# A hybrid retention and window-attention layer on one core: new queue figures in the order's planner, one store for each retention output, two x blocks held in SBUF, query and key rows in one DRAM array

## The chip, the core and the metric

The kernel runs on one core of a Trainium2 chip. Its time is device time in microseconds (us) for one execution. Three timed runs of the kernel before gave 704.1, 706.53 and 708.13 us, so its median is 706.53 us. The profile comes from one further execution.

## The reference, cut to what matters

```python
def reference(x, norm_w, w_in, ret_norm_w, q_norm_w, k_norm_w, sinks, rel_bias, w_out):
    h = rms_norm(x, norm_w)                                  # x: 1 x 2048 x 1024, float32
    proj = einsum('bsd,de->bse', h, w_in)                    # 2816 columns
    rq, rk, rv, rg, sq, sk, sv, sg = split(proj, [256, 256, 512, 512, 512, 128, 128, 512])
    rq, rk = rotary(rq), rotary(rk)                          # 4 heads of 64
    ro = retention(rq, rk, rv)                               # 4 heads, 128 values each, decay gamma per head
    ro = group_norm(ro) * ret_norm_w * silu(rg)
    so = sliding_window_attention(sq, sk, sv, q_norm_w, k_norm_w, sinks, rel_bias)   # window 128
    so = so * silu(sg)
    return x + einsum('bse,ed->bsd', concat([ro, so]), w_out)

def retention(q, k, v):                                      # by chunks, state carried along
    scores = (q_c k_c^T) * decay
    out = scores v_c + (q_c * xi) state
    state = gamma^C * state + (k_c * zeta)^T v_c
```

Everything is float32, and the output has the shape of x.

## The kernel before, in words

**The four large products.** The projection is cut into three column groups (1024, 768 and 1024 columns) and the output projection is the fourth product. A float32 operand is split into a high part and a remainder (tiles `hi` and `lo`, in the profile `x<-x` and `w<-w`: ScalarE makes the high part, VectorE the remainder), and TensorE does three passes on the parts. Each product goes by a seven-product scheme (`STEPS`, m = 1 to 7) over eight pairs of 128-token chunks, so one projection is 7 x 8 blocks of 4 x 3 matmuls, 672 in all. In the profile they are `acc<-w,x`, with 512 columns of the moving operand, 384 in the second projection.

**What lies between them.** The second, third and fourth product share TensorE with the window attention (`window`, `attend`, `values`) and the retention (`retention`, `keys_of`, `update`, `retain`, `group_norm`), whose plain float32 matmuls are the `m<-...` rows. The names that matter below: `qT` and `ks` are queries and keys of the window attention, `lg` its logits, `pm` the exponentials, `pT` their transposes, `so` its output; `a` is the tile of query and key rows before the rotary step, `qk` and `qkT` what comes of it, `sT` the decayed scores of the retention (VectorE multiplies the scores in PSUM by the mask `dm`), `ro` its outputs; `g` are gate columns, `go` a gated output on its way into the last product. `apart` is a tile rearranged by ScalarE for a transpose by DMA through `planes_dram`.

**What goes through DRAM.** The second projection's rows go to two arrays `rq0_dram` and `rq1_dram` of 384 columns each. `keys_of` reads query and key rows back in two loads (384 columns from the first, 128 from the second). x is loaded from `in_xt` for the first product and its blocks m = 1, 2 and 4 again for the second and third (`kept_blocks`); four sums are kept in `s0_dram` to `s3_dram`. `retain` works on two chunks at once. Its two PSUM banks per head pair are filled so that ScalarE copies each out in one instruction of all 128 partitions (`ro<-m` 128x256); in the tile `ro` half of the rows then belong to the other head and the other half chunk. After the group norm, three stores of 64 partitions for each `ro` tile (one of 256 columns, two of 128) put them in their places in `ro_dram`. Since rows are crossed, the inverse norms are needed crossed too: two small DMAs fill `rstd_crossed`.

**What sets the order.** Every step is recorded by `op` with a cost for each engine that can do it, the buffers that it reads and writes, and a due time in units of blocks of the large products. `Program.emit` then picks step after step: it keeps a time at which each engine is free, a pool of 93 buffers of 128x512 (tag `k`) with a ceiling per use (`SHARE`), and a model of the DMA queue, which is SyncE's (SP, in the planner `Q`). The order that comes out is written into the program for each engine and holds on the chip, however long a step takes there: an instruction that waits keeps back all that stand behind it on its engine, on SP too. In the program each DMA on SP waits, besides what it needs, for the landing of the DMA eight places ahead of it.

The queue's model before: a transfer of `kb` KB takes `0.15 + kb / 450` us of a common bus, lands 2.6 us after that, and the next may be issued after 0.45 us and not before the bus is within `BACKLOG` = 1.5 us:

```python
bus = max(bus, s) + occ
free[e] = max(s + more, bus - BACKLOG)
o.end = bus + lat
```

A buffer that a planned step gives back is used again from the planned end on (`slots`), so a store that lands later than planned holds up the step that gets its buffer next.

Of the kernel before, what the change touches and what calls it, by code (L numbers as in the profile page):

```python
# [29 lines left out]
F32 = mybir.dt.float32  # L30
# [30 lines left out]

AHEAD_OF = {"x": 3.0, "wh": 8.0}
# [23 lines left out]
BACKLOG = 1.5  # L86
# [48 lines left out]
class Program:  # L135
# [33 lines left out]
    def emit(self):  # L169
# [16 lines left out]
        done, now = 0, 0.0  # L186
        while done < count:
            best = None
            for e, found in avail.items():
# [4 lines left out]
                for due, n, o in found[:48]:  # L194
# [13 lines left out]
                    if shared and e != "Q":  # L208
                        s = max(s, port)
# [47 lines left out]
            if e == "Q":  # L257
                occ, lat, more = o.cost[e]
                bus = max(bus, s) + occ
                free[e] = max(s + more, bus - BACKLOG)  # L260
                o.end = bus + lat
            else:
# [50 lines left out]
TURN = (1.8, 2.7, 1.35)  # L313
# [21 lines left out]
def both(n):  # L335
    return {"V": dve(n, True)}
# [21 lines left out]
def dma(kb, issue=0.45):  # L358
    return {"Q": (0.15 + kb / 450, 2.6, issue)}
# [3 lines left out]
VALUES = {P: dma(256, 0.6), 96: dma(192, 0.6), 32: dma(64, 0.63)}  # L363
# [30 lines left out]
def layer(ctx, tc, xt, xfirst, xtok, nw, w_in, w_rn, qkw, sinks, biasg, rope, decays, dmask, gpow, w_out, out):  # L394
# [34 lines left out]
    def fixed(shape, name, dtype=F32):  # L429
        return Buf(name=name, ap=const.tile(shape, dtype, name=name))  # L430
# [56 lines left out]
    rstd_crossed = fixed([P, NCH], "rstd_crossed")  # L487
    crossed = [Part(rstd_crossed, lambda t: t) for _ in range(2)]
    made, held_up = [[], []], Buf(name="held_up", ap=())
# [14 lines left out]
    rq_dram = [scratch([P, 384], f"rq{n}_dram", NCH) for n in range(2)]  # L504
    g_dram = scratch([P, 512], "g_dram", NP)
    ro_rows = dram.tile([NCH, P, 512], F32, name="ro_dram")
    ro_parts = []
    for c in range(0, NCH, 2):
        made_of = [[], []]
        for pr in range(2):  # L510
            at_rows = lambda u, lo, n, c=c, pr=pr: ro_rows[c : c + 2, HALVES[u], pr * 256 + lo : pr * 256 + lo + n]
            made_of[pr].append((Buf(name="ro_dram", ap=at_rows(0, 0, 256).rearrange("k t (x d) -> t k x d", x=2)), HALVES[pr], None))
            for x in range(2):
                made_of[pr].append(
                    (Buf(name="ro_dram", ap=at_rows(1, (1 - x) * P, P).rearrange("k t d -> t k d")), HALVES[1 - pr], x)
                )
        ro_parts.append(made_of)
# [160 lines left out]
    def kept_blocks(base, seq):  # L678
# [6 lines left out]
        for m, p in seq.all:  # L685
            due = base + seq.at[m, p]
            t = kb("x", "raw")
            load(t, of[m](p), due - 2.5)
            B[m, p] = split(t, 512, due - 0.6, "x", "x")
# [187 lines left out]
    def retention(at):  # L877

        for i, half in enumerate(HALVES):
            op(  # L880
                dma(8), lambda e, i=i, half=half: e.dma_start(rstd_crossed()[half, :], rstd_all()[HALVES[1 - i], :]),
                [rstd_all], [crossed[i]], at(0) - 12, label="crossed", also=(rstd_crossed,),
            )
        for t, heads, r in ((0, slice(0, 2), (rstd_all,)), (0, slice(2, 4), tuple(crossed)), (1, slice(0, 4), (rsq_all,))):
            by = rstd_crossed if len(r) == 2 else r[0]
            part = Part(factors[t], lambda a, heads=heads: a[:, :, heads])
            made[t].append(part)
            op(
                {"V": (0.25, 0.33, True)},
                lambda e, part=part, by=by, t=t, heads=heads: e.tensor_tensor(  # L890
                    part(), dec()[:, t : t + 1, heads].to_broadcast([P, NCH, heads.stop - heads.start]),
                    by().unsqueeze(2).to_broadcast([P, NCH, heads.stop - heads.start]), ALU.mult,
                ),
                [dec, *r], [part], at(0) - 9, label="factors", also=(factors[t],),
            )
        op(
            {"V": (0.25, 0.33, True)}, lambda e: e.tensor_tensor(squares(), factors[0](), factors[0](), ALU.mult),
            made[0], [squares], at(0) - 9, label="factors",
# [779 lines left out]
```

## Time and profile before

| | before |
|---|---|
| timed runs, us | 704.1, 706.53, 708.13 (median 706.53) |
| the profiled execution's own time, us | 703.36 |
| its span, first to last instruction, us | 701.6 |
| mean granted TensorE clock | 0.995 |
| TensorE matmul busy, us (share) | 685.6 (98%) |
| VectorE, ScalarE, GpSimd busy, us | 604.6, 475.5, 42.5 |
| HBM traffic | 106.64 MB read, 56.69 MB written |

1.7 us of the execution's own time lie outside the span. "Busy" of TensorE is the union of the matmuls' durations, which overlap, so the 16.0 us of the span that are left are time in which no matmul was in flight. One line number, 390, stands for nearly all instructions, because a helper records them; groups are told apart by their tiles. A row `A <- B` in the view of waits says that engine and tile A were released last by B.

### The profile page before, as it was taken

The numbers are of one execution on the slowest core, as the hardware profiler recorded it, in microseconds if no ns is written. First come the engines' busy times: TensorE is split into PE (matmuls) and PEld (weight loads), VectorE is DVE, ScalarE is ACT, GpSimd is POOL, SyncE is SP. The second block draws the span as 40 slices with busy tenths as digits, with TensorE's granted clock in tenths as the row PEclk, the third lists the DMA queues.
The fourth block names the chain that finished last, engine by engine and source line by source line (L and its number), as shares of the span: only waits on it lengthen the run. The fifth ranks groups of instructions, "written<-read, shape, count | busy, mean of one in ns | idle before, by whom it ended". The sixth has DMA issues, their size and how long they took to land.

```text
span 701.6 us, 15585 instructions
## 1 busy us (share of the span) xinstructions
PE 685.6 (98%) x5428; PEld 578.6 (82%) x5428; DVE 604.6 (86%) x1483; ACT 475.5 (68%) x1122; POOL 42.5 (6%) x75
## 2 busy tenths in 40 slices
PE   9999999999999999999989989999989999999998
PEld 7888888889999999986768767888768788788886
DVE  6999887877999979899988879899787799999962
ACT  7666965656896666979768958995989844253300
POOL 1000000025020001102000000100000000000000
PEclk9999999999999999999999999999989999999999
DMA  9999955989977699999999899699799898315822
GB/s 321 365 342 335 384 179 182 348 270 297 330 194 229 198 302 312 262 323 273 321 268 320 199 266 308 136 269 316 190 316 304 193 290 272 105 45 172 279 102 93
DMA packets 171487, 179.07 MB, mean 255 GB/s; under 512 B 71824, under 2 KB 106768, under 8 KB 171408
## 3 DMA queue, kind: packets, MB, share of 16 engines
q1 hardware_dynamic: 171264, 178.07, 83.9%
q8 instruction: 43, 0.70, 0.4%
q14 instruction: 36, 0.29, 0.1%
q10 hardware_dynamic: 144, 0.00, 0.0%
HBM read 106.64 MB, written 56.69 MB: 233 GB/s over the span
## 4 chain that ended last, share of the span: by engine, by line
PE 75%; DVE 14%; DMA 6%; ACT 2%; issue 2%; SPq 0%; DVEq 0%; ACTq 0%
PE acc L390 64%; PE m L390 10%; DVE x L390 4%; DVE w L390 2%; DVE lg L390 2%; DVE go L390 2%; DMA g<-g_dram 2%; ACT ro L390 1%; DVE t L390 1%; DMA planes_dram<-apart 1%; DVE s L390 1%; DMA w<-in_w_out 1%; DMA x<-s_dram 1%; DMA vd<-aq_dram 1%; DMA so_dram<-so 1%
## 5 line engine op out<-in xcount | busy, mean ns | idle before, releaser
L390 PE MATMUL acc<-w,x 128*128 128x512 f32 (+1 forms) x2700 | 594.9, 379 | 2.2 <-DVE x L390 1.2
L390 PEld LDWEIGHTS acc<-w,x 128*128 128x128 f32 x2700 | 493.7, 189 | 87.1 <-issue 3.2
L390 DVE TENSOR_TENSOR x<-x 128x512 fp32r<-128x512 f32 (+2 forms) x220 | 148.0, 695 | 17.3 <-ACT x L390 17.0
L390 ACT ACTIVATE x<-x 128x512 fp32r<-128x512 f32 (+1 forms) x187 | 111.8, 618 | 15.0 <-DVE x L390 7.2
L390 DVE TENSOR_TENSOR w<-w 128x512 fp32r<-128x512 f32 (+3 forms) x96 | 61.8, 669 | 2.5 <-ACT w L390 2.4
L390 ACT ACTIVATE pm<-lg,nm 128x128 f32<-128x128 f32 x128 | 50.0, 401 | 7.1 <-DVE lg L390 7.1
L390 ACT ACTIVATE w<-w 128x512 fp32r<-128x512 f32 (+1 forms) x72 | 41.0, 603 | 20.2 <-DVE w L390 11.3
L390 DVE CUSTOM_DVE_ANT_0 lg<-m,bias,nsnk 128x160 f32<-128x160 f32 x128 | 42.7, 383 | 8.7 <-PE m L390 8.6
L390 DVE SCALAR_TENSOR_TENSOR w<-w,nw_sb 128x512 fp32r<-128x512 f32 (+3 forms) x72 | 49.1, 706 | 1.0 <-ACT w L390 0.9
L390 DVE TENSOR_TENSOR s<-acc,s 128x512 f32<-128x512 f32 (+1 forms) x64 | 42.1, 657 | 6.9 <-PE acc L390 6.6
L390 POOL TENSOR_SCALAR_AFFINE_SELECT own<-pT 64x512 f32<-64x512 f32 x32 | 25.4, 806 | 258.0 <-ACT pT L390 239.4
L390 DVE TENSOR_TENSOR t<-acc,t 128x512 f32<-128x512 f32 (+2 forms) x33 | 21.2, 642 | 19.9 <-PE acc L390 19.4
L390 ACT ACTIVATE x<-go 128x512 fp32r<-128x512 f32 x40 | 24.2, 626 | 13.7 <-DMA w<-in_w_out 3.6
L390 DVE TENSOR_TENSOR x<-go,x 128x512 fp32r<-128x512 f32 x40 | 27.7, 699 | 3.5 <-ACT x L390 3.5
L390 ACT ACTIVATE s<-acc 128x512 f32<-128x512 f32 (+1 forms) x32 | 17.9, 565 | 18.6 <-PE acc L390 13.6
L390 ACT ACTIVATE w<-w,nw_sb 128x512 fp32r<-128x512 f32 (+3 forms) x44 | 28.2, 682 | 3.0 <-DMA w<-in_w_in 1.8
L390 ACT ACTIVATE apart<-qn 128x1024 uint16<-128x1024 uint16 x16 | 16.9, 1054 | 19.4 <-DVE qn L390 19.3
L390 ACT ACTIVATE ro<-ro,nmu,rg 128x128 f32<-128x128 f32 x64 | 25.2, 486 | 1.1 <-DVE nmu L390 1.1
L390 DVE TENSOR_TENSOR t<-acc,s 128x512 f32<-128x512 f32 (+1 forms) x32 | 21.2, 663 | 5.0 <-PE acc L390 5.0
L390 ACT ACTIVATION_READ_ACCUMULATOR pm<-lg,nm 128x1 f32 x128 | 25.4, 199 | 0.0
L390 ACT ACTIVATE xk<-xk 128x512 f32<-128x512 f32 x32 | 19.9, 623 | 5.9 <-DMA xk<-in_xtok 5.8
L390 PE MATMUL m<-ks,qT 64*32 64x160 f32 x1024 | 23.2, 300 | 0.6 <-issue 0.6
(133 smaller groups left out, 663.6 us busy)
## 6 DMA issues: line engine op xcount, KB each, us to landing
x<-in_xt SPq DMA_DIRECT2D x80, 256.0 KB, 4.8
x<-s_dram SPq DMA_DIRECT2D x64, 256.0 KB, 4.7
planes_dram<-apart SPq DMA_DIRECT2D x56, 256.0 KB, 4.7
w<-in_w_in SPq DMA_DIRECT2D x40, 256.0 KB, 4.8
s_dram<-x SPq DMA_DIRECT2D x32, 256.0 KB, 4.6
xk<-in_xtok SPq DMA_DIRECT2D x32, 256.0 KB, 5.5
res<-in_xtok SPq DMA_DIRECT2D x32, 256.0 KB, 4.4
w<-in_w_out SPq DMA_DIRECT2D x20, 256.0 KB, 5.6
```

The costliest lines, as they stand in the source:

```text
L390: return lambda *a, **k: self.order.put(op(*a, **k))
```

## The change

It has four parts.

- **The queue's model in the planner.** `BACKLOG` goes. A transfer now starts on the bus `FETCH` = 0.3 us after its issue, the queue is held until the transfer eight places ahead has landed (`LANES` = 8), a transfer takes `0.16 + kb / 440` us and lands 2.5 us after, and issuing takes 0.55 us in place of 0.45. The figures of a transpose by DMA change from (1.8, 2.7, 1.35) to (1.6, 2.5, 1.65). These numbers move instructions on every engine.
- **Retention outputs in one transfer.** The matmuls of `retain` use the banks by head (`banks[i]` for `banks[i ^ u]`), with masks and decays laid out to fit. For the second head pair ScalarE crosses the two halves of the partitions while it copies out of PSUM, in four instructions of 64 partitions in place of two of 128. A `ro` tile is stored in one DMA of 128 partitions. `rstd_crossed` and its two DMAs go, and with them one of the small VectorE instructions that make `factors`.
- **Two x blocks kept.** `HELD` = 2: the high and low parts of the first two x blocks of the second projection stay in four of the 93 buffers until the third projection has used them, which then has two loads and two splits fewer.
- **Query and key rows in one array.** `rq0_dram` and `rq1_dram` become one array of 768 columns, and `a` is filled by one load of 512 columns.

```diff
+HELD = 2
+FIRST_X, SPLIT_X = 2.5, 0.6
+SHARE["held"] = 2 * HELD
...
-BACKLOG = 1.5
+LANES, FETCH = 8, 0.3
...
-                    if shared and e != "Q":
+                    if e == "Q":
+                        s = max(s, landings[-LANES] if len(landings) >= LANES else 0.0)
+                    elif shared:
                         s = max(s, port)
...
-                bus = max(bus, s) + occ
-                free[e] = max(s + more, bus - BACKLOG)
+                bus = max(bus, s + FETCH) + occ
+                free[e] = s + more
                 o.end = bus + lat
+                landings.append(o.end)
...
-TURN = (1.8, 2.7, 1.35)
+TURN = (1.6, 2.5, 1.65)
...
-def dma(kb, issue=0.45):
-    return {"Q": (0.15 + kb / 450, 2.6, issue)}
+def dma(kb, issue=0.55):
+    return {"Q": (0.16 + kb / 440, 2.5, issue)}
...
-    rq_dram = [scratch([P, 384], f"rq{n}_dram", NCH) for n in range(2)]
+    rq_rows = dram.tile([NCH, P, 768], F32, name="rq_dram")
...
+            if again and (m, p) in held:
+                B[m, p] = again[m, p]
+                continue
...
-        load(a0, rq_dram[0][c], soon - 3, 192, also=(a,))
-        load(a1, rq_dram[1][c], soon - 3, 64, also=(a,), of=lambda t: t[:, 0:128])
+        op(
+            dma(256), lambda e: e.dma_start(a(), rq_rows[c, :, 0:512]), [rq_dram[0][c], rq_dram[1][c]], [a], soon - 3,
+            label="load a",
+        )
...
-                                    banks[i ^ u][pr]()[HALVES[u ^ pr], k * P : (k + 1) * P], qkT()[r, o : o + 64],
+                                    banks[i][pr]()[HALVES[u ^ pr], k * P : (k + 1) * P], qkT()[r, o : o + 64],
...
-                            h, o = 2 * pr + (u ^ x), (2 * k + pr) * 64
+                            h, o = 2 * pr + x, (2 * k + pr) * 64
...
             for x in range(2):
...
-                op({"A": act(256)}, go, [banks[x][pr]], [ro], due + 0.7, label="ro")
+                for half, to in ((slice(0, P), slice(0, P)),) if pr == 0 else zip(HALVES, HALVES[::-1]):
+                    part = Part(ro, lambda t, x=x, to=to: t.rearrange("p (k x d) -> p k x d", k=2, x=2)[to, :, x, :])
+                    parts.append(part)
+                    op(
+                        {"A": act(256)},
+                        lambda e, part=part, out=banks[x][pr], half=half: e.activation(
+                            part(), out()[half, 0:256].rearrange("p (k d) -> p k d", k=2), AF.Copy
+                        ),
+                        [banks[x][pr]], [part], due + 0.7, label="ro", also=(ro,),
+                    )
...
-            for to, rows, x in ro_parts[c // 2][pr]:
...
-                op(dma(128 if x is None else 64), go, [ro], [to], due + 0.6, label="store ro")
+            store(ro_dram[c // 2][pr], ro, due + 0.6, 280, of=lambda t: t.rearrange("p (k d) -> p k d", k=2))
...
-    B1 = kept_blocks(n7, TWOS)
+    B1 = kept_blocks(n7, TWOS, TWOS.all[:HELD])
...
-    B3 = kept_blocks(2 * n7, TWOS)
+    B3 = kept_blocks(2 * n7, TWOS, TWOS.all[:HELD], B1)
```

TensorE has the same instructions in both programs, in other places. SP has 750 DMAs in place of 802: 32 fewer `ro_dram<-ro`, 16 fewer `a<-rq_dram`, 2 fewer `x<-in_xt` and the 2 of `rstd_crossed`. ScalarE has 16 more `ro<-m` and 2 fewer `x<-x`, VectorE 2 fewer `x<-x`.

The first place is SP's queue near the last retention group, where the gate columns `g` are loaded. Before, the rows are:

```order
L390 DMA ro_dram<-ro 64x2x128 x2
L390 DMA ro_dram<-ro 64x2x256
L390 DMA ro_dram<-ro 64x2x128 x2
L390 DMA_TRANSPOSE r<-planes_dram 128x4x256
L390 DMA go<-ro_dram 128x512 x2
L390 DMA go<-so_dram 128x512
L390 DMA w<-in_w_out 128x512
L390 DMA go<-ro_dram 128x512 x2
L390 DMA w<-in_w_out 128x512 x3
L390 DMA planes_dram<-apart 128x1024
L390 DMA x<-s_dram 128x512
L390 DMA g<-g_dram 128x512
```

Now they are:

```order
L397 DMA w<-in_w_out 128x512
L397 DMA ro_dram<-ro 128x2x256
L397 DMA w<-in_w_out 128x512
L397 DMA_TRANSPOSE r<-planes_dram 128x4x256
L397 DMA ro_dram<-ro 128x2x256 x2
L397 DMA w<-in_w_out 128x512 x2
L397 DMA x<-s_dram 128x512
L397 DMA go<-ro_dram 128x512 x2
L397 DMA g<-g_dram 128x512
L397 DMA planes_dram<-apart 128x1024
L397 DMA go<-so_dram 128x512
L397 DMA go<-ro_dram 128x512 x2
```

Twelve stores of `ro` became four, the four loads of the last product's weights moved ahead of the gate loads, and this `g`, the seventh of eight, stands directly behind the ninth and tenth `go<-ro_dram` instead of eight DMAs later.

The second place is TensorE where the retention begins, early in the third projection; `m<-ks,qT` are logits of the window attention, `m<-ident,pm` transposes of its exponentials, `m<-ident,kn` a transpose of keys. Before, the rows are:

```order
L390 MATMUL m<-v,qk 64x128 x16
L390 MATMUL m<-ks,qT 32x160 x16
L390 MATMUL m<-ident,pm 128x128 x8
L390 MATMUL acc<-w,x 128x512 x3
L390 MATMUL m<-ident,kn 128x128
L390 MATMUL m<-ks,qT 32x160 x16
L390 MATMUL acc<-w,x 128x512 x3
L390 MATMUL m<-ident,pm 128x128 x4
L390 MATMUL acc<-w,x 128x512 x3
L390 MATMUL m<-ident,pm 128x128 x4
L390 MATMUL acc<-w,x 128x512 x30
```

Now they are:

```order
L397 MATMUL m<-v,qk 64x128 x16
L397 MATMUL m<-ks,qT 32x160 x16
L397 MATMUL m<-ident,pm 128x128 x8
L397 MATMUL acc<-w,x 128x512 x21
L397 MATMUL m<-ident,kn 128x128
L397 MATMUL acc<-w,x 128x512 x48
L397 MATMUL m<-state,qkT 64x128 x12
L397 MATMUL m<-qkT 64x64 x16
L397 MATMUL acc<-w,x 128x512 x9
L397 MATMUL m<-v,sT 64x128 x16
L397 MATMUL acc<-w,x 128x512 x15
L397 MATMUL m<-ks,qT 32x160 x16
```

The next group of logits stood 3 matmuls of the large product behind the transposes; now 93 of them lie between.

The third place is ScalarE at one of the retention's copies out of PSUM. Before, the rows are:

```order
L390 ACTIVATE qk<-qk,factors_83 128x64 x4
L390 ACTIVATE apart<-qk 128x1024
L390 ACTIVATE ro<-m 128x2x128 x4
L390 ACTIVATE x<-x 128x512
L390 ACTIVATE w<-w 128x512
```

Now they are:

```order
L397 ACTIVATE qk<-qk,factors_82 128x64 x4
L397 ACTIVATE ro<-m 128x2x128 x2
L397 ACTIVATE ro<-m 64x2x128 x4
L397 ACTIVATE apart<-qk 128x1024
L397 ACTIVATE x<-x 128x512
```

Four copies became six, and here they stand ahead of the rearranging step instead of behind it.

87 lines of the change are left out of this document (32 added, 55 removed).

## Prediction

> **What bounds the kernel now.** I read the page first.
>
> ```profile
> PE 685.6 (98%) x5428; PEld 578.6 (82%) x5428; DVE 604.6 (86%) x1483; ACT 475.5 (68%) x1122; POOL 42.5 (6%) x75
> ```
>
> TensorE is busy for 98% of the span and the change leaves its instructions as they are, so its work is a floor; what can move is the time that it waits, or runs at a lower clock. The view of waits, for TensorE alone, has eight rows:
>
> ```profile
> PE m L390 <- ACT pT L390: 3.9, 2, 2.1
> PE m L390 <- DVE sT L390: 3.3, 1, 3.3
> PE m L390 <- DVE none L390: 1.3, 1, 1.3
> PE acc L390 <- DVE x L390: 1.2, 3, 0.7
> PE acc L390 <- ACT x L390: 1.0, 1, 1.0
> PE m L390 <- DVE go L390: 0.8, 1, 0.8
> PE m L390 <- issue: 0.6, 1, 0.6
> PE m L390 <- ACT pm L390: 0.4, 2, 0.2
> ```
>
> Without the opening (`none`, 1.3) they sum to 11.2 us. Windows of 25 us say where, and what the clock did (columns: window, length, busy time and instructions of PE, PEld, DVE, ACT, POOL, granted clock, DMA share, GB/s):
>
> ```profile
> 50.00:75.00 25.00, 25.00 (x112) 20.71 (x111) 24.67 (x42) 19.14 (x50) 0.00 (x0) 1.00 0.98 340
> 350.00:375.00 25.00, 22.68 (x267) 18.07 (x266) 21.34 (x60) 16.81 (x44) 1.61 (x2) 1.00 1.01 271
> 400.00:425.00 25.00, 22.47 (x342) 17.13 (x333) 19.69 (x74) 15.43 (x36) 1.45 (x2) 1.00 1.04 284
> 500.00:525.00 25.00, 21.36 (x172) 16.85 (x171) 21.32 (x39) 22.02 (x38) 0.00 (x0) 0.87 0.99 286
> 525.00:550.00 25.00, 25.00 (x116) 20.58 (x115) 16.28 (x46) 22.55 (x42) 0.00 (x0) 0.99 0.91 247
> ```
>
> The first product runs without a gap although the DMA engines are as busy there as anywhere. The gaps lie between 325 and 560 us, where attention and retention are slotted in. One of them also lowers the clock: 25 x 0.13 + 25 x 0.01 = 3.5 us of clock are missing around 520 us. About 0.5 us of that fell while TensorE waited anyway, so 3.0 us count. The ceiling of what better order can win is 11.2 + 3.0 = 14.2 us, 2.0%.
>
> Next, what ends each wait last. The largest one, by the chain of waits in a window (start, us, what):
>
> ```profile
> 509.58 6.19 DMA g<-g_dram
> 515.77 0.02 issue
> 515.79 0.03 ACT g L390
> 515.82 0.60 issue
> 516.42 0.72 ACT w L390
> 517.16 0.06 DVE w L390
> 517.83 0.68 DVE t L390
> 518.52 0.66 DVE w L390
> 519.18 0.35 DVE sT L390
> 519.57 1.98 PE m L390 x32
> ```
>
> TensorE needs `sT`. VectorE has its two `sT` behind four `w`, these need ScalarE's `w`, and ScalarE stood for a load of gate columns. The largest wait on `x` and the two on `pT`, these with ScalarE's row ahead, from the timeline (the bracket is the idle time before and its releaser):
>
> ```profile
> 327.27 0.74 PE L390 MATMUL acc<-w,x 128*128 128x512 f32 x2 [1.00 <-ACT x L390]
> 365.62 0.60 ACT L390 ACTIVATE s<-acc 128x512 f32<-128x512 f32 x1 [3.10 <-DMA so_dram<-so]
> 366.76 0.66 PE L390 MATMUL m<-ident,pm 128*128 128x128 f32 x4 [1.76 <-ACT pT L390]
> 412.85 0.60 ACT L390 ACTIVATE pT<-m 128x512 f32<-128x512 f32 x1 [4.78 <-DMA planes_dram<-apart]
> 413.50 1.09 PE L390 MATMUL m<-pT,vs 128*64 128x128 f32 x14 [2.15 <-ACT pT L390]
> ```
>
> At `pT` ScalarE both times got a buffer whose last user was a store that had not landed: the planner took it for free too early. So 3.9 + 3.3 + 0.8 (`go`, a load of `ro_dram`) of the 11.2 us, and the clock's 3.0, go back to DMAs that landed later than planned. The 2.2 us on `x` are another kind; the largest piece is the 1.00 us at 327 us, where logits and exponentials crowd ScalarE and VectorE.
>
> **The queue's figures.** The median times from issue to landing, with the size, of some issues:
>
> ```profile
> a<-rq_dram SPq DMA_DIRECT2D x16, 192.0 KB, 4.6
> ro_dram<-ro SPq DMA_DIRECT2D x16, 128.0 KB, 2.6
> ro_dram<-ro SPq DMA_DIRECT2D x32, 64.0 KB, 2.1
> so_dram<-so SPq DMA_DIRECT2D x16, 256.0 KB, 4.0
> ```
>
> The old model lands 256 KB 0.72 + 2.6 = 3.3 us after issue when idle, and with its backlog of 1.5 us at most about 4.8 us; `g` above took 6.19. The new one lands it after 0.3 + 0.74 + 2.5 = 3.5 us when idle and, with eight in flight, after 8 x 0.74 = 5.9 us. That is nearer. What it is worth: the two waits on `pT` are worth 0 to 3.9 us; I take half, 2.0, since the buffer is again the one with the earliest planned end. The new order has moved 93 matmuls between two groups of logits early in the retention, which thins the crowd behind the 2.2 us on `x`; 0 to 2.2, I take 1.5, as the releasers there are VectorE and ScalarE themselves.
>
> **Retention outputs.** The stores first:
>
> ```profile
> 493.94 7.82 SPq L390 DMA_DIRECT2D ro_dram<-ro  x12
> L390 SPq DMA_DIRECT2D ro_dram<-ro x48: 574/605/1446, 389.2 to 550.9; - x48
> 505.33 0.79 SPq L390 DMA_DIRECT2D go<-ro_dram  x2
> ```
>
> A 64-partition store holds SP for 0.605 us, a load for 0.79 / 2 = 0.4. Of 48 stores 16 remain, so SP is free for 32 x 0.605 = 19.4 us more, and eight of those 32 were in the twelve issued 8 to 16 us ahead of the late `g`. That is 8 x 0.605 = 4.8 us there, and `g` is also eight DMAs earlier relative to the `go<-ro_dram` beside it. If `g` comes in time, ScalarE's wait of 1.5 us goes:
>
> ```profile
> 515.79 0.72 ACT L390 ACTIVATE g<-g,rstd_all 128x512 f32<-128x512 f32 x1 [1.51 <-DMA g<-g_dram]
> ```
>
> TensorE's wait then falls from 3.3 to 1.8 us. What is late next is VectorE's queue of `w` ahead of `sT`, which stands there still. Waits of 1.76 and 2.15 us, above, lie in windows with a clock of 1.00, so at 1.8 the clock's 3.0 us go too: together 4.5 of 6.3, between bounds of 0 and 6.3. The wait on `go` gets 0.5 of its 0.8, because loads of `ro_dram` are no longer behind triples of stores.
>
> The Trainium skill ("TensorE: Matmul & The Clock Gate", HAM oscillation) puts the limit for idle gaps at about 3.4 us, on a free-running window. The wait of 3.28 us here did halve the clock; by the skill as by the rows 1.8 us would not.
>
> ScalarE pays for it:
>
> ```profile
> L390 ACT ACTIVATE ro<-m 128x256 f32<-128x256 f32 x32 | 9.5, 379 | 0.0
> L390 ACT ACTIVATE x<-x 128x512 fp32r<-128x512 f32 (+1 forms) x187 | 111.8, 618 | 15.0 <-DVE x L390 7.2 <-PE acc L390 5.4 <-DVE w L390 1.2
> ```
>
> A copy costs 9.5 / 32 = 0.30 us in a row of them. No 64-partition copy is in the trace; the work per partition is the same 256 elements, so I take 0.30 each, 16 x 0.30 = 4.8 us more, 0.6 for each pair of chunks. It can cost nothing, where TensorE waits for neither `ro` nor what follows, or all 4.8, where it does; no gain, because no copy goes. ScalarE runs 15.4 to 22.6 of 25 us in these windows, and no wait on `ro` stands among TensorE's rows, so I take 1.0. The Trainium skill ("ScalarE: Activation LUTs", Rules for kernel authors) speaks more strongly against the change: about 0.3 us per ACTIVATE and 0.83 ns per element, 0.51 us for each copy and 8.2 us in all as an estimate. By that the term would be 1.7 in place of 1.0. The row has 0.30 us for the whole instruction, and I keep to it. VectorE loses one small instruction and SP two tiny DMAs, worth nothing under the 98%.
>
> **x blocks kept.** Two splits of 111.8 / 187 = 0.6 us on ScalarE, their two remainders on VectorE and two loads go. In this stretch of 125 us in the second projection TensorE has no gap:
>
> ```profile
> 150.00:275.00 125.00, 125.00 (x1265) 118.59 (x1264) 110.38 (x328) 89.83 (x249) 20.16 (x31) 1.00 0.89 264
> ```
>
> So loads and splits of this kind are covered by TensorE's own work. Without that cover two would be worth 2 x 0.6 = 1.2 us, and as they leave shortly ahead of the crowd at 327 us, that much of the 1.5 for `x` may be theirs; I count nothing more. The price is 4 of 93 buffers for the length of the second projection: 0, or one more wait for a buffer of the size of the two above, 2.0; I take 0.5, as there is no wait at all there now.
>
> **One load for `a`.** 16 loads fewer, for 16 x 0.4 = 6.4 us of SP's time. The rotary step waited for both loads before and waits for the one now; 192 KB took 4.6 us and 256 KB of other kinds 4.0 to 6.2. Nothing, within 0.3 either way.
>
> **New waits.** A new order puts new instructions ahead of one another, and the trace of before cannot show which. Its own order, planned by wrong figures, has 3.9 + 3.3 + 1.2 + 1.0 = 9.4 us of waits on `pT`, `sT` and `x`; I take about a fifth of that, 2.0, since half of its causes are the figures that are mended. The bounds are 0 and one wait like that on `sT` with its clock, 6.3.
>
> **The sum.** Against the profiled execution: -2.0 (`pT`) - 1.5 (`x`) - 4.5 (`sT` and clock) - 0.5 (`go`) + 1.0 (copies) + 0.5 (buffers) + 2.0 (new waits) = -5.0, so 703.36 - 5.0 = 698.4 us. The median of the timed runs, 706.53, lies 3.2 above that execution; I carry the difference over and forecast 706.53 - 5.0 = 701.5 us. 0.5% of it, 3.5 us, is about what a measurement of this kernel can tell from no change.
>
> **Rivals.** *The waits only move.* Landing times vary, as 2.1 to 6.2 us in the rows above show, and no fixed figure foresees them; removed waits of 8.5 us come back as others of 4 to 10. For it: five separate places waited before, each for a reason of its own. Against: four of the causes are the same one. Time: 706.53 - 8.5 + 7 + 1.5 = 706.5, within 0.5%. That the held blocks and the single load do nothing belongs here, as they are hidden either way.
>
> *A second clock drop.* The six copies per pair of chunks, ahead of `apart` or `x`, make ScalarE the late one at a `pT` or `x`, in windows where it already ran 22.0 to 22.6 of 25 us. Two copies more, 0.6 us, on top of a wait of 2.15 make 2.75; with one late store it passes 3.3, and from there the clock halves. The price is 3.3 + 3.0 = 6.3 us, and 1.5 for copies and buffers stays. With half of the gains (4.2 of 8.5) the time is 706.53 + 6.3 - 4.2 + 1.5 = 710.1, with a quarter (2.1) 712.2. For it: TensorE's `sT` is still only 6 matmuls behind its scores and VectorE's `w` still ahead of it. Against: SP's 19.4 and 6.4 us of relief lie in this stretch.
>
> **How the numbers follow.** Forecast, faster by over 0.5%: 0.56, with 693 to 703 as its own range. Waits only move: 0.24, at 703 to 710. A second clock drop: 0.20, at 710 to 712.2. Full success is 706.53 - 14.2 = 692.3. The range from 692.5 to 711 leaves out the far half of the last case and next to nothing below. Faster 0.56, same 0.24, slower 0.20.
>
> **What would show it.** Right: no row `PE <- ACT pT` with `DMA planes_dram` or `so_dram` behind ScalarE's idle time; at the last `sT` a wait under 2 us and a clock of 1.00 in every window from 300 to 600 us; SP with 16 rows `ro_dram<-ro`; TensorE's waits after the opening summing to about 6 to 8 us. Wrong: a sum of waits of 11 us or more in other places, a window with a clock under 0.95, or TensorE waiting for `ro` or for a buffer in the second projection. If the copies of 64 partitions take more than 0.4 us each, that term was too small.

## The result, and the profile after

The changed kernel takes 688.6 us (median of four runs, 687.99 to 688.87), the kernel before beside it 705.61 us (704.1 to 708.13): a ratio of 0.9754, interval 0.9722 to 0.9786, or 17.0 us. That is below the forecast of 701.5 us and below the range (692.5 to 711). The profiled execution took 688.87 us, with a span of 687.1 us, 14.5 us less than before. The other 2.5 us of the 17.0 are no gain of that execution: the runs of before have their median 2.2 us above its profile, those of the changed kernel 0.3 us below.

The page's row of busy time, and the three rows that the view of TensorE's waits has in the changed kernel:

```profile
PE 679.3 (99%) x5428; PEld 577.9 (84%) x5428; DVE 604.5 (88%) x1479; ACT 481.5 (70%) x1137; POOL 43.1 (6%) x75
```

```profile
PE m L397 <- ACT pm L397: 2.9, 1, 2.9
PE m L397 <- DVE none L397: 1.3, 1, 1.3
PE acc L397 <- DVE x L397: 0.2, 1, 0.2
```

Seven rows after the opening, 11.2 us, have become two, 3.1 us. That is 8.1 of the 14.5. Most of the rest is in the first row: TensorE's busy time fell from 685.6 to 679.3 us, 6.3 us, for the same 5428 matmuls. The clock does not explain it, as the windows show (columns as in the prediction):

```profile
350.00:375.00 25.00, 24.93 (x402) 20.11 (x395) 24.26 (x99) 20.19 (x65) 3.60 (x4) 1.00 1.11 314
400.00:425.00 25.00, 22.77 (x335) 18.01 (x327) 23.56 (x95) 24.65 (x63) 1.80 (x2) 1.00 0.94 244
425.00:450.00 25.00, 24.14 (x114) 19.72 (x116) 22.03 (x49) 21.54 (x53) 1.55 (x2) 0.86 0.62 193
500.00:525.00 25.00, 25.00 (x205) 20.48 (x204) 23.50 (x59) 24.88 (x43) 0.00 (x0) 1.00 1.11 305
525.00:550.00 25.00, 25.00 (x114) 20.71 (x113) 20.91 (x39) 23.65 (x44) 0.00 (x0) 1.00 1.09 309
```

The gap at 500 to 525 us, which had the largest wait and the low clock, is gone (25.00 busy, clock 1.00). One clock drop remains, at another place: 25 x 0.14 = 3.5 us of clock are missing behind 425 us, as much as before. So the 6.3 us are stalls that the view of waits cannot see. The next row says how they hide: matmuls of the large product, by shape.

```profile
L397 PE MATMUL acc<-w,x 128*128 128x512 f32 x2004 | 467.5, 393 | 0.2 <-DVE x L397 0.2
```

A matmul is shown with 393 ns, but 2004 of them cover 467.5 us, 233 ns each. Each lasts some 160 ns into the next one, so a matmul that starts 160 ns late, or the first 160 ns of any longer stall, leaves no idle time. From both traces I took the time from each matmul's start to the next start, less the median for that pair of tiles and shapes in the same trace, and added up the differences of more than 0.1 us: 30.6 us before, 16.4 us after. These sums hold the waits and the clock's loss too; they differ by 14.2 us, nearly all of the span's 14.5.

The stores, with the time that each holds SP (minimum, median and maximum in ns), and ScalarE's copies:

```profile
L397 SPq DMA_DIRECT2D ro_dram<-ro x16: 359/393/1520, 386.2 to 535.2; - x16
L397 ACT ACTIVATE ro<-m 64x256 f32<-64x256 f32 x32 | 12.1, 379 | 0.6
L397 ACT ACTIVATE ro<-m 128x256 f32<-128x256 f32 x16 | 5.1, 373 | 0.1
```

A store of 128 partitions and 256 KB holds SP for 0.39 us, less than one of 64 partitions and 64 or 128 KB did (0.605). A copy takes 373 or 379 ns by either shape, but in a row those of 128 partitions overlap (before 9.5 us for 32, 0.30 each) and those of 64 do not (12.1 for 32, 0.38 each). ScalarE has 12.1 + 5.1 - 9.5 = 7.7 us more, not 4.8. The Trainium skill's estimate in the prediction (8.2 us, from "ScalarE: Activation LUTs", Rules for kernel authors) comes near that only by chance: its price is that of an ACTIVATE whose bias is a pointer operand, which these copies are not given, and 0.51 us for each copy is not what the row shows.

The wait that remains, by the chain of waits in its window:

```profile
421.81 1.34 ACT pm L397 x7
423.15 0.03 issue
423.18 0.66 ACT ro L397 x2
423.84 0.02 issue
423.86 0.38 ACT ro L397
...
425.04 0.38 ACT ro L397
425.42 0.39 ACT pm L397 x2
425.81 0.04 issue
425.86 1.71 PE m L397 x6
```

TensorE stands for the exponentials `pm`, and between the first four and the next ScalarE makes all six copies of a pair of chunks. The wait is 2.93 us, and the clock halves behind it. This is nearly the mechanism of the rival "a second clock drop" (there the six copies made a `pT` or `x` late, here it is `pm`, and no late store is needed), inside a kernel that is 17 us faster.

### The profile page after: what moved, and what is told of

It reads as the page before. It is cut to its first block, busy times and chain, and to the rows that moved or that the text cites. A ratio compares the mean times of both kernels' runs of the same rounds, so it can differ in the third digit from the quotient of the medians.

```text
span 687.1 us, 15551 instructions
## 1 busy us (share of the span) xinstructions
PE 679.3 (99%) x5428; PEld 577.9 (84%) x5428; DVE 604.5 (88%) x1479; ACT 481.5 (70%) x1137; POOL 43.1 (6%) x75
## 4 chain that ended last, share of the span: by engine, by line
PE 96%; ACT 2%; DVE 1%; DMA 1%; issue 0%; DVEq 0%; ACTq 0%
PE acc L397 83%; PE m L397 13%; ACT ro L397 1%; DMA ro_dram<-ro 1%; DVE lg L397 0%; ACT pm L397 0%; DVE sT L397 0%; DVE x L397 0%; DVE qn L397 0%; DVE tsin L397 0%; ACT w L397 0%; DVE tcos L397 0%; DVE w L397 0%; DVE qk L397 0%; DVE t L397 0%
## 5 line engine op out<-in xcount | busy, mean ns | idle before, releaser
L397 DVE TENSOR_TENSOR x<-x 128x512 fp32r<-128x512 f32 (+2 forms) x218 | 145.7, 690 | 9.4 <-ACT x L397 9.3
L397 ACT ACTIVATE x<-x 128x512 fp32r<-128x512 f32 (+1 forms) x185 | 109.7, 614 | 20.8 <-DVE x L397 16.7
L397 DVE TENSOR_TENSOR w<-w 128x512 fp32r<-128x512 f32 (+3 forms) x96 | 60.4, 653 | 3.2 <-ACT w L397 3.1
L397 DVE TENSOR_TENSOR t<-acc,t 128x512 f32<-128x512 f32 (+2 forms) x33 | 21.1, 639 | 16.6 <-PE acc L397 16.4
L397 ACT ACTIVATE c<-acc 128x512 f32<-128x512 f32 (+1 forms) x24 | 13.4, 560 | 15.9 <-PE acc L397 14.2
L397 DVE TENSOR_TENSOR r<-acc,t 128x512 f32<-128x512 f32 (+1 forms) x32 | 20.8, 651 | 3.5 <-PE acc L397 3.4
```

The costliest lines, as they stand in the source:

```text
L397: return lambda *a, **k: self.order.put(op(*a, **k))
```

## The experiments

Two theories stood against each other at first. *Queue figures*: the planner now knows when DMAs land, so buffers and loads come in time; the stores matter at one or two places. *Stores*: 48 small stores held up everything behind them on SP, and with 16 the order hardly matters. A third came up on the way: *planned price*, that the planner, charged for 48 stores, makes a bad order. All runs, with the kernel before on the same chip (medians of 702.81 to 705.61 us):

| run | queue figures | stores planned / issued | other | median us (range) | ratio, interval |
|---|---|---|---|---|---|
| before | old | 48 / 48 | | 705.61 (704.1–708.13) | 1 |
| changed | new | 16 / 16 | held blocks, one `a` load | 688.6 (687.99–688.87) | 0.9754, 0.9722–0.9786 |
| m1 | new | 48 / 48 | | 714.97 (713.24–716.43) | 1.0172, 1.0135–1.0209 |
| m2 | old | 16 / 16 | held, one load | 697.66 (694.38–700.16) | 0.9919, 0.9891–0.9946 |
| m3 | old | 16 / 16 | | 693.85 (691.9–695.48) | 0.9879, 0.9845–0.9912 |
| m4 | new | 48 / 48 | held, one load | 707.61 (704.38–711.64) | 1.0077, 1.0048–1.0106 |
| m5 | new | 16 / 16 | one load | 687.92 (687.13–689.05) | 0.977, 0.9747–0.9793 |
| m6 | new | 16 / 16 | held | 693.15 (689.55–697.12) | 0.9846, 0.9798–0.9894 |
| m7 | new | 48 / 48 | changed, six copies | 704.82 (702.77–710.87) | 1.0023, 0.9997–1.0048 |
| m8 | old | 48 on GpSimd | | 697.33 (694.87–699.64) | 0.9903, 0.987–0.9936 |
| n1 | new | 16 / 48 | changed | 699.73 (695.68–701.91) | 0.9934, 0.9907–0.9961 |
| n2 | new | 48 / 16 | changed | 700.92 (699.55–702.26) | 0.9948, 0.9921–0.9975 |
| n3 | new | 16 / 16 | | 689.8 (687.67–691.42) | 0.9803, 0.9757–0.9849 |
| `FETCH` 0.35 | new | 16 / 16 | changed | 689.26 (689.14–690.12) | 0.9801, 0.9753–0.9849 |
| n5 | old | 48 / 16 | six copies | 694.18 (692.72–695.87) | 0.9841, 0.9787–0.9894 |
| n6 | new | 16 / 16 | changed, four copies | 684.9 (683.37–685.9) | 0.9706, 0.9654–0.9759 |
| n7 | new | 16 / 16 | changed, copies later | 688.52 (688.19–691.54) | 0.9773, 0.9709–0.9838 |
| n8 | new | 16 / 16 | changed, copies late, old price | 686.93 (686.39–687.29) | 0.9737, 0.9686–0.9787 |
| n9 | new | 16 / 16 | n8 without held blocks | 688.77 (687.06–689.53) | 0.9776, 0.9751–0.9801 |
| n10 | new | 16 / 16 | changed, again | 688.5 (686.18–688.93) | 0.9772, 0.9746–0.9798 |

### Which part carries the gain

m1 is the kernel before with the first part of the change alone, m4 the changed kernel without the second part, m3 the second part alone, m2 the changed kernel without the first:

```diff
# m1, and missing in m2 and m3
-BACKLOG = 1.5
+LANES, FETCH = 8, 0.3
# m3, and missing in m1 and m4
-            for to, rows, x in ro_parts[c // 2][pr]:
+            store(ro_dram[c // 2][pr], ro, due + 0.6, 280, of=lambda t: t.rearrange("p (k d) -> p k d", k=2))
```

> The kernel before with the new queue model alone (48 small stores of the retention outputs, no held blocks, two loads of the query and key rows). Queue theory (the gain comes from an order that fits the landings): two thirds of the gain or more, 691 to 695 us, and no TensorE wait behind a late store. Transfer theory (the gain comes from fewer and larger DMAs): 703 to 707. Chance theory (any new order scatters the waits): anywhere from 688 to 706, with no pattern over the four runs.

> The changed kernel with the old queue model, the other three parts kept. Queue theory: 701 to 707 us, with waits behind DMAs as in the kernel before. Transfer theory: 688 to 693. Chance theory: anywhere from 688 to 706.

> The kernel before with the retention outputs crossed by ScalarE and stored in one DMA, nothing else. Queue theory: 703 to 708 us. Transfer theory: 691 to 697, since 34 of the 52 DMAs go here. Chance theory: anywhere from 688 to 706.

> The changed kernel with the retention outputs as before: four ScalarE copies for each pair of chunks, three stores for each tile. Queue theory: 683 to 690 us, because the wait of 2.9 us behind six copies and its half clock can go. Transfer theory: 698 to 704. Chance theory: anywhere from 688 to 706.

The queue figures alone make the kernel 1.7% slower. The merged stores alone give 8.9 us against the kernel before on their chip (702.81), with the old figures and their old errors; the wait on `sT` does not come back, and 0.3 us on `pT` is left. Without them (m4) the other three parts leave the kernel slower than before. So the theory of the queue figures falls as a cause by itself. But m2 says that the figures are worth something where the stores are merged: 697.66 without, 688.6 with. m1's view of TensorE's waits has one row of a size that no kernel with 16 planned stores has:

```profile
PE acc L393 <- ACT x L393: 15.7, 3, 14.4
```

It lies at 583 us, at the start of the last product, and m4 has its like, 9.1 us at 576.

m5 drops the held blocks, m6 goes back to two arrays and two loads for `a`:

```diff
# m5
-    B1 = kept_blocks(n7, TWOS, TWOS.all[:HELD])
+    B1 = kept_blocks(n7, TWOS)
# m6
-            dma(256), lambda e: e.dma_start(a(), rq_rows[c, :, 0:512]), [rq_dram[0][c], rq_dram[1][c]], [a], soon - 3,
+        load(a0, rq_dram[0][c], soon - 3, 192, also=(a,))
+        load(a1, rq_dram[1][c], soon - 3, 64, also=(a,), of=lambda t: t[:, 0:128])
```

> The changed kernel with HELD = 0: the third projection loads and splits all its x blocks. Store theory (the 48 small stores of the retention outputs, and the order planned around them, cost nearly all of the difference): 687 to 692 us. Chance theory (any new order scatters the waits): anywhere from 688 to 700.

> The changed kernel with two DRAM arrays and two loads for the query and key rows. Store theory: 687 to 692 us. Theory of the DMA count (each of the 52 DMAs saved is worth the same): 16 of 52 come back, a third of the gain, 692 to 695.

In the time the held blocks are worth nothing that can be told (687.92 against 688.6), but the traces do tell. TensorE's two waits on `x` at 325 us, the first of which the prediction showed for the kernel before, are back in m5, and the clock drops behind them:

```profile
325.63 0.74 PE L393 MATMUL acc<-w,x 128*128 128x512 f32 x2 [1.14 <-ACT x L393]
327.17 0.80 PE L393 MATMUL acc<-w,x 128*128 128x512 f32 x1 [0.80 <-DVE x L393]
325.00:350.00 25.00, 23.57 (x233) 18.82 (x234) 23.02 (x71) 21.11 (x58) 1.52 (x2) 0.93 1.12 302
```

All eight kernels without held blocks (before, m1, m3, m5, m8, n3, n5, n9) have this pair, of 1.0 to 1.2 and 0.7 to 0.8 us, and none of the twelve with them has it. The order of TensorE goes the same way: groups of logits 9 and then 3 matmuls of the large product apart stand there in those eight alone. m5's time is no worse because its order happens to lack the wait of 2.9 us on `pm`. The single load looks like 4.5 us in m6, but n3 below has neither part and takes 689.8, only 1.9 us above m5 and 1.2 above the changed kernel. The single load cannot be told from what another order brings.

### The stores on the chip, or their price in the plan

m7 is the changed kernel with three stores of 64 partitions in place of each one; m8 is the kernel before with its 48 stores given to GpSimd:

```diff
# m7
-            store(ro_dram[c // 2][pr], ro, due + 0.6, 280, of=lambda t: t.rearrange("p (k d) -> p k d", k=2))
+            for to, r, lo, n in ro_dram[c // 2][pr]:
...
+                op(dma(128 if n == 256 else 64), go, [ro], [to], due + 0.6, label="store ro")
# m8
-                op(dma(128 if x is None else 64), go, [ro], [to], due + 0.6, label="store ro")
+                op({"G": (1.0, 3.5, False)}, go, [ro], [to], due + 0.6, label="store ro")
```

> The changed kernel with each retention output tile stored in three DMAs of 64 partitions, as before; ScalarE still crosses the halves. Store theory: 700 to 712 us, with a wait of 5 to 15 us between 570 and 590 us, as the two kernels with the new model and 48 stores had it. Layout theory (banks by head and the crossing copies bring the gain): 687 to 692.

> The kernel before with its 48 stores issued by GpSimd, which is idle for 93% of the span, and nothing else changed. If the price of the stores is SP's time and its eight places: 692 to 698 us, about what the kernel with merged stores alone reached. If it is the transfers' own time on the DMA engines: 700 to 706. The order changes too, so chance can blur it by some 3 us.

m7 gives back the whole gain with nothing changed in the program but the number of stores. m8 gains 6.3 us by taking the same small stores off SP, although there they hold GpSimd for as long and land later (4.8 and 5.3 us after issue, in place of 2.6 and 2.1):

```profile
L390 POOL DMA_DIRECT2D ro_dram<-ro x48: 590/592/795, 386.8 to 541.4; - x48
ro_dram<-ro POOLq DMA_DIRECT2D x16, 128.0 KB, 4.8
ro_dram<-ro POOLq DMA_DIRECT2D x32, 64.0 KB, 5.3
```

This points at SP's queue as what pays. m8 does not show that a late landing is free, since its planner was told of 3.5 us there, and its order changed too. The Trainium skill ("DMA: Bandwidth & Descriptors", Rules for kernel authors) says that transfers of the two partition halves run one after the other on the same engines and are better made as one of 128 partitions, and that spreading DMAs over other queues saves issue time alone. The advice to make one transfer agrees with n1 below (11.1 us), and m8's 6.3 us fit a price in issue time; that the halves run one after the other no run here shows.

In m7 the order changes with the stores, since the planner is charged for them. n1 keeps the changed kernel's order on every engine and issues three stores where one is planned; n2 keeps m7's order and issues one where three are planned:

```diff
# n1
+                for r, lo, n in ((HALVES[0], 0, 256), (HALVES[1], 0, P), (HALVES[1], P, P)):
...
+                    e.dma_start(to, ro()[r, :].rearrange("p (k d) -> p k d", k=2)[:, :, lo : lo + n])
# n2
+                def go(e, ro=ro, to=to, n=n):
+                    if n == 0:
+                        e.dma_start(to(), ro().rearrange("p (k d) -> p k d", k=2))
```

> The changed kernel, whose order still has one planned store for each retention output, but each is issued on the chip as three stores of 64 partitions (48 in all). Every engine keeps the changed kernel's order. Theory "stores on the chip": the 32 additional stores hold SP for 32 x 0.605 - 16 x 0.22 = about 16 us more in the retention stretch and delay the loads behind them; the time goes to 700 to 705 us, and waits of TensorE on x, acc or sT behind DMAs appear. Theory "the planned price": the time of 704.82 with three planned stores came from the order that the planner makes when each is charged; with the order kept, 688 to 693 us and no wait of over 4 us at 575 us.

> The order of the kernel with three stores for each retention output (704.82 us), but on the chip each output is issued as one store of 128 partitions at the place of the first of the three. Theory "stores on the chip": the wait of 12.9 us at 574 us goes with the stores, 687 to 693 us. Theory "the planned price": the wait stands in the order itself, ahead of which VectorE works without a pause; it stays at 9 to 13 us, and the time is 699 to 705 us.

Neither theory had it alone. From 688.6 the stores on the chip cost 11.1 us (n1), the order planned for them 12.3 us (n2), both together 16.2 us (m7). The expectation for n1 has a sign wrong: by the medians, 48 small stores hold SP for 48 x 0.605 = 29.0 us and 16 merged ones for 16 x 0.393 = 6.3, so the difference is 22.8 us and not 16.

How the stores cost time is seen in n1, where every other instruction stands as in the changed kernel (the sum of late starts, 16.4 us there, is 28.1 us here). Its TensorE waits, the four largest:

```profile
PE acc L397 <- ACT so L397: 3.8, 1, 3.8
PE m L397 <- ACT pm L397: 2.5, 1, 2.5
PE m L397 <- DVE sT L397: 2.5, 1, 2.5
PE acc L397 <- DVE s L397: 1.8, 1, 1.8
```

SP in n1 just ahead of 500 us, and the chain of waits that follows from it to the last `sT`:

```profile
496.84 3.89 SPq L397 DMA_DIRECT2D ro_dram<-ro  x6
```

```profile
504.89 6.65 DMA go<-ro_dram
511.54 0.02 issue
511.56 0.69 DVE go L397
...
516.58 1.32 DVE w L397 x2
517.90 0.34 DVE sT L397
518.25 0.04 issue
518.29 1.22 PE m L397 x32
```

Six stores take SP 3.9 us; in the changed kernel two do in 1.0 us. The loads behind them go out later, VectorE stands for `go`, and `sT` is late behind it. This is the place, and with 2.5 us nearly the size, of the `sT` wait of before. The first row, 3.8 us on `so`, comes by another way. The chain there, and the same store in the changed kernel:

```profile
397.64 4.04 DMA ro_dram<-ro
...
401.81 0.70 DVE qn L397
402.51 0.02 issue
402.53 1.06 ACT apart L397
403.59 0.02 issue
403.61 0.61 ACT so L397
404.22 0.04 issue
404.26 0.79 PE acc L397
```

```profile
391.85 5.40 DMA ro_dram<-ro
```

`qn` gets the buffer of an `ro` tile and must wait until the last store out of it has landed. The three stores do not hold the tile longer: from the issue of the first (396.37 us) to the landing of the last they take 5.3 us, the one of the changed kernel 5.4. They start 4.5 us later, behind nine small stores on SP where three merged ones stood, and `qn` starts 4.5 us later (401.81 against 397.35). So here too it is SP's queue that pays: small stores delay what stands behind them, loads and other stores alike. Both ways end at TensorE in waits that halve the clock: n1's granted clock is 0.93 in the windows from 400 and from 500 us, about 3.5 us together. A third window of 0.93, from 425 us, lies behind the wait on `pm`, which the changed kernel has as well.

n2's cost is mostly one wait, like m1's, m4's and m7's, at 569 us (TensorE's waits after the opening sum to 13.0 us in n2 and 3.1 in the changed kernel, 9.9 of the 12.0 us between their spans):

```profile
PE acc L397 <- ACT x L397: 11.8, 1, 11.8
```

The chain behind it is VectorE working for the last 14 us, with pauses of less than 0.5 us. Counted up to the start of the matmul that waits, the 4925th, VectorE has begun 1347 instructions in n2 and 1326 in the changed kernel; 36 matmuls earlier the counts were 1313 and 1312. The additional 21, about 21 x 0.6 = 13 us, are mostly gated outputs `go` and weights `w` of the last product (11 and 4 more). TensorE needs what stands behind them. That this order comes from the planned price is shown by n1 and n2, which differ in it; why the planner's rules choose it was not tried.

n5 asks the same of the old figures: m3 with three stores planned and one issued.

```diff
# n5, in m3
-            store(ro_dram[c // 2][pr], ro, due + 0.6, 280, of=lambda t: t.rearrange("p (k d) -> p k d", k=2))
+            for n, to in enumerate(ro_dram[c // 2][pr]):
...
+                op(dma(64 if n else 128), go, [ro], [to], due + 0.6, label="store ro")
```

> The kernel before with its old queue figures; ScalarE crosses the partitions in six copies, the planner is charged for three stores of each retention output, and one store of 128 partitions is issued on the chip. Theory "stores on the chip": as the merged stores alone, 692 to 696 us. Theory "the planned price": the order stays that of 48 stores, 703 to 707 us. If each carries a part, as with the new figures, 697 to 701.

694.18 us, as m3 (693.85). With the old figures, whose small stores are cheaper, the plan for 48 stores is as good as the one for 16, and the stores on the chip are the whole gain, 9.9 us against before on that chip (704.05) with the dearer copies already paid. The bad order arises only where the new figures price 48 stores.

### What the six copies cost

n6 keeps the changed kernel's order, but copies the second head pair in two instructions of 128 partitions. It leaves out the crossing, so values in the retention half of the output stand in wrong places; only its time is of use. n7 and n8 keep the six copies and let them come later:

```diff
# n6
-                            part(), out()[half, 0:256].rearrange("p (k d) -> p k d", k=2), AF.Copy
+                            ro().rearrange("p (k x d) -> p k x d", k=2, x=2)[:, :, x, :],
+                            out()[:, 0:256].rearrange("p (k d) -> p k d", k=2), AF.Copy
# n7 and n8
-                        [banks[x][pr]], [part], due + 0.7, label="ro", also=(ro,),
+                        [banks[x][pr]], [part], due + 2.0, label="ro", also=(ro,),
# n7 only
-                        {"A": act(256)},
+                        {"A": act(256) if half.stop - half.start == P else (0.39, 0.5, False)},
```

> The changed kernel with its order, but the second head pair is copied out of PSUM in two instructions of 128 partitions instead of four of 64 (its rows stay uncrossed, so the retention half of the output has head and chunk halves in wrong places; all else is as in the changed kernel). If the six copies cause the wait of 2.9 us at 425 us and its half clock, the wait falls to about 2.1 us or less and the time to 681 to 686 us. If the copies are hidden and the wait has another cause, 687 to 689.

> The changed kernel with the copies out of PSUM due 2.0 units instead of 0.7 after their block, and those of 64 partitions priced at the measured 0.39 us. If copies ahead of the exponentials are what the changed kernel still pays for, no wait of TensorE behind a row of six copies, clock 1.00, 683 to 687 us. If not, or if another wait comes in its place, 688 to 695.

> As the one with later copies, but at the old price, so only the due time moves. 683 to 687 us if lateness of the copies alone frees the exponentials; 688 to 695 if the order just has another wait.

n6 is 3.7 us below the changed kernel, and its row for the remaining wait reads

```profile
PE m L397 <- ACT pm L397: 0.7, 1, 0.7
```

with no window under a clock of 1.00. Two copies of 64 partitions less at that place, and 2.2 us of wait and the clock's 3.5 us are gone. Not all 5.7 show in the time, and the timed runs of the changed kernel had clocks of 0.995 to 0.998. n7 and n8 lose the wait too (0.3 and 0.5 us on `pm`), and n8's 686.93 is the lowest median of all but n6. n7 is no faster than the changed kernel, and its clock drops at the same place, to 0.94 from 400 to 425 us, although no wait of TensorE there is over 0.81 us.

### How much an order by itself is worth

n3 is m3 with the new figures (the first and second part alone); the next is the changed kernel with a slightly different figure; n9 joins n8 with m5; n10 is the changed kernel once more, on n9's chip.

```diff
# FETCH 0.35
-LANES, FETCH = 8, 0.3
+LANES, FETCH = 8, 0.35
# n9, beside n8's edit
-HELD = 2
+HELD = 0
```

> The kernel before with the new queue figures and the merged retention stores, without held blocks and without the single load of query and key rows. If the queue figures are worth something with 16 stores, it lies below the 693.85 us of the merged stores alone: 687 to 690. If held blocks and single load make the difference, 692 to 695. If such differences of some us are the luck of one order, anywhere from 688 to 698.

> The changed kernel with FETCH = 0.35 in place of 0.3 in the planner's queue model, an immaterial change that gives another order. Theory "a single order is luck of some us": the time differs from 688.6 by 2 to 8 us with the same work. Theory "the figures themselves matter": 688 to 690, as the figure is nearly the same.

> The changed kernel with the copies out of PSUM due later (2.0 units) and no held x blocks. Held blocks alone were worth about nothing (687.92 without them against 688.6) and late copies 1 to 2 us (686.93). If the two add, 685 to 687 us; if an order's own luck is larger than both, 688 to 692.

> The changed kernel itself once more, beside the one above on the same chip. 688 to 689 us if chips agree; then the kernels of other calls can be compared with it directly.

The changed kernel repeats within 0.1 us (688.6 and 688.5), so times from different chips are compared here as they are. Without n6, kernels with new figures and 16 stores planned and issued lie between 686.9 and 689.8 us, but for m6 (693.15), and with the old figures at 693.85, 694.18 and 697.66. So the new figures are worth 4.1 us (m3 to n3) to 9.1 us (m2 to the changed kernel) once the stores are merged. If m6's 4.5 us are the doing of an order, a difference of that size between two kernels says little, and only the 9.1 stands clear of it. n8 with its range of 686.39 to 687.29 overlaps that of n10, 686.18 to 688.93. No version with the right output clearly beats the changed kernel.

## Why the prediction was wrong, point by point

The direction was right, the size was not: -5.0 us forecast, -14.5 in the profiled execution and -17.0 in the medians. The step that failed is the term of the **retention outputs**. I had worked out that SP becomes free for 19.4 us, and then counted it at one place, the late `g` ahead of `sT`, and the wait on `go`: 5.0 us together. At that place the direction was right. Issuing the 48 stores again in the same order (n1) costs 11.1 us: the `sT` wait comes back, and beside it come waits on `so` (behind stores that start 4.5 us later on SP) and on `s`, and two more drops of the clock. The 19.4 us were too low as well, since a merged store holds SP for 0.39 us and not 0.605; by the measured medians it is 22.8. A second term was too small beside it: with the stores merged, the queue figures were worth 4.1 to 9.1 us.

- **The ceiling** of 14.2 us, from which the range's lower end came, was wrong. It added up the idle time that the view of waits shows. TensorE's busy time fell by 6.3 us at the same work and a like clock, so stalls too short to show were there to be won as well.
- **`pT`, -2.0**: the waits went, 3.9 us, so half was too little. The figures can do it as predicted: with them and 48 stores no such row is left (m1, m4, m7). The merged stores do most of it too, since with the old figures 0.3 us (m3) or 1.4 us (n5) is left. Over the whole kernel the figures alone do harm (m1).
- **`x`, -1.5**: 2.0 of 2.2 us went, but not by the new figures. The crowd of logits was thinned, as predicted, only in kernels with held blocks, and the two waits at 325 us stand in all eight kernels without them.
- **`sT` and clock, -4.5**: the wait of 3.3 us went whole, and so did the low clock at 520 us; VectorE's queue of `w` was not late next. So the step that 1.8 us would be left and would not lower the clock was not put to the test here; in m2 a wait of 1.80 us is followed by a drop.
- **Copies, +1.0**: too small, for the one place where TensorE comes to wait behind them. ScalarE's additional time was 7.7 us and not 4.8, and the place at `pm` costs 3.7 us by n6. The prediction's own mark, 0.4 us for each copy, was nearly reached.
- **Buffers, +0.5, and the held blocks**: no price is seen. I gave the blocks at most 1.2 us of the term for `x`; by the traces they take away the whole pair of waits, 1.7 to 2.0 us, though the times of m5 and the changed kernel do not show it.
- **New waits, +2.0**: the one that came is that of the copies; no other was left.
- **The rivals.** *The waits only move* did not happen: 11.2 us became 3.1. *A second clock drop* had its mechanism nearly right, six copies on a ScalarE that is 24.65 of 25 us busy and a halved clock, but its price stands against a gain three times what I allowed. Where I was furthest from the mark is a case that I did not have: the queue figures slower by themselves, by an order that is 12 us late at one place.
- **The 3.2 us** between the profiled execution and the median, carried over to the forecast, were not carried over by the changed kernel: its median lies at its profile.

Left open: whether the small stores cost by SP's 0.6 us each or by the rule that a DMA waits for the one eight places ahead of it, as 32 DMAs fewer ease both. It was not tried, since the rule stands in the program's waits.

## What to carry to other kernels

Where one queue issues all transfers, count small DMAs by what they hold of the queue over the whole stretch, not by the one wait in which they can be seen; and if TensorE is 98% busy, take the ceiling from the starts of its matmuls, not from its idle time. A planner with better figures is not safe by itself: the same figures were worth 4 to 9 us with 16 stores and cost 12 us with 48 (m1 against the kernel before on its chip), so test such a table together with the program that it orders, and change the program first.

## What the runs showed of the hardware

- A store of 64 partitions held SP for 0.605 us (median of 48), one of 128 partitions with two to four times the bytes for 0.39 us (median of 16).
- The same copies out of PSUM took 0.30 us each in a row at 128 partitions and 0.38 us at 64 partitions crossing over, at the same 256 elements per partition.
- The granted clock, which the traces record as full or half, fell to half behind waits of 2.93 us (changed kernel) and 2.58 us (n10); the windows behind them have 0.86 and 0.93. It also fell behind shorter ones: 1.80 us in m2, the pair of 1.14 and 0.80 us in m5, and 0.81 us, with 0.32 us shortly before, in n7. It did not fall behind 1.76 and 2.15 us in the kernel before. So no length of a single wait divides the two in these runs. The rows of n10, m2 and n7, each with the window of its drop:

```profile
425.62 1.48 PE L397 MATMUL m<-ident,pm 128*128 128x128 f32 x6 [2.58 <-ACT pm L397]
425.00:450.00 25.00, 24.27 (x136) 19.59 (x140) 22.96 (x50) 22.24 (x53) 1.56 (x2) 0.93 0.68 198
```

```profile
479.35 3.10 PE L394 MATMUL acc<-w,x 128*128 128x512 f32 x7 [1.80 <-ACT x L394]
475.00:500.00 25.00, 23.20 (x116) 18.54 (x115) 19.97 (x39) 23.89 (x39) 0.00 (x0) 0.93 1.09 305
```

```profile
422.13 0.64 PE L397 MATMUL m<-state,qkT 64*64 64x128 f32 x2 [0.81 <-PE m L397]
400.00:425.00 25.00, 23.44 (x415) 17.95 (x417) 22.43 (x96) 21.13 (x63) 2.44 (x3) 0.94 0.65 182
```

The Trainium skill's limit for idle gaps, about 3.4 us ("TensorE: Matmul & The Clock Gate", HAM oscillation), is above all of them, and above the 3.28 us of before; these runs do not bear it out. In the prediction I took waits under about 3 us to be safe; they are not.
